# A hybrid decoder step: scan rows kept in SBUF, memory values split from PSUM, earlier scan loads, other PSUM banks

## The chip, the cores and the metric

The kernel runs on one core of a Trainium2 chip. The metric is the device time of one execution in microseconds (us). A median of the runs is compared; the profile is of one further execution.

## The reference, cut to what matters

One layer of a decoder on 1024 prompt tokens and 8 x 4 sample tokens, width 1024, all in float32. A normalized input is projected onto columns for three branches; their outputs are concatenated (3072 wide) and projected back, with a residual and a last norm.

```python
hn = rmsnorm(x, norm_g)
gm_uv, gm_gate, ssm_z, ssm_xbc, ssm_dt, mem_q, mem_gate = split(hn @ w_in)
a_out, v_rows = gmlp_branch(gm_uv, ...)            # gelu, layernorm, 128x128 mixing
a_out = a_out * silu(gm_gate)
b_out, ssm_new, conv_new = mamba2_branch(ssm_z, ssm_xbc, ssm_dt, ...)
c_out = memory_branch(mem_q, mem_gate, mem_k, mem_v)  # 4 heads x 256, 256 memory rows
y = x + concat([a_out, b_out, c_out]) @ w_out
```

`mamba2_branch` is a causal convolution and a scan over chunks of 128 tokens: for each of 16 heads a decay matrix times `C B^T`, times `x dt`, plus the carried state; then a gate with `silu(z)`, a norm over each of two groups of 512 columns, and a gain. For the prompt `mem_k` and `mem_v` are computed from 256 memory rows and are outputs; for the samples they come from a cache, and the scan starts from a given state.

## The kernel before, in words

Every float32 product is made of three products of rounded operands: each operand is split into a high part H (a copy rounded to float32r, mostly on ScalarE) and a low part L (the difference, mostly on VectorE): `split`, lines 121 to 127. TensorE computes HH + HL + LH (`gemm3`, lines 335 to 345).

The order of all instructions is written by hand. The main stream is the large products. Side work is a queue of Python generators (`Side`); after every three products a hook adds a rate (`set_pace`) to a counter, and at each whole number one step of the first generator is written into the program, up to its next `yield`. All engines run their instructions in that order. SP issues nearly all DMAs, GpSimd a few. A DMA that has to wait (for data, or for its buffer) holds what stands behind it on its queue.

The main stream: columns of z, v; then units of 256 columns. A fast unit (`unit`, line 495) is seven products of 512-wide blocks with four k each, 28 hooks; a plain unit (`unit_plain`, line 555) eight, 32 hooks. Six units are convolution columns, then four of q, two of the memory gate (mg), four of the gMLP gate (gg), four of u; then plain units: two of mg and four of the first third of the output projection (written to `y_d`). A weight block is split group by group, three groups ahead (`u_split`, line 441); its low part is left for the next hook (`u_late`, line 452). In each unit the 32 sample columns are products into a bank `U.bank()` (`samp_in`, line 483), copied to `se`, and in the next unit transposed into another bank (`samp_out`, line 470).

PSUM has eight banks of 128x512: three `mm` for the main products, one `acc`, four `sd` for everything beside.

Side chains. `side_chain` (line 1748, begun by `conv_end` in the first q unit): `conv_samples`, `sample_scan` (line 1343; 8 states of 128x1024, each scaled on GpSimd in `s1`, line 1431), a wait for the flag `F_.q` set by `q_there` in the first mg unit, `sample_scores`, `sample_values`, `mem_prep` (line 1649: norm and transposes of the memory rows, H and L stored to `mem_d`), and `gm_prep` (line 1683: spatial weights). `scan_chain` (line 1932) is begun by `scan_open` in the first plain mg unit: `decay_rows` (line 909; rows of `Lraw` through SP, rows of `Rt` through GpSimd), then `scan` (line 1231): 16 chunks (group g, chunk c). For each, `sA` transposes x and B, `sE` makes the decay (a product of Lt and Rt, then ScalarE), `sM` multiplies it by `C B^T`, `sXsplit` splits x times decay (ScalarE, then GpSimd for `xdL`), lines 1201 to 1203 form the state, line 1276 the diagonal part; `gate_norm` gates and norms y; one iteration later `y_T` transposes it into an `sd` bank and `y_T2` scales it (ScalarE, line 1124) and stores it to `yb_d`.

After the plain units: 16 products for keys and values of the memory (blk 0 to 7, two halves each; lines 2070 to 2089). Beside them `loadB` and `splitB` load y from `yb_d`, at most three tiles ahead, and split it into bH and bL; `splitB` is called once per product and twice at every fourth. Values go to `mv_d` and are read back as `vr`, to be split in the attention chain. Then `outproj` (line 1973): 24 products (192 hooks) that add to `y_d`, with `attention` (line 2171) as side chain at pace 0.38, which in the end loads c, x rows, the last gain and y sums for the last stage.

`a_split` (line 1946) splits the gMLP output, four blocks, beside the second plain mg unit: two halves of 128x1024 each, the low parts through `u_late`.

Of the kernel before, what the change touches and what calls it, by code (L numbers as in the profile page):

```python
# [58 lines left out]
def hybrid_step(ctx, tc, x_prompt, x_sample, mem_prompt, state_ssm, state_conv, cache_mem_k,  # L59
# [355 lines left out]
    U.bank = acc_bank  # L415

# [24 lines left out]
    def u_split(u, j):  # L441
# [7 lines left out]
        U.late.append((l, src, h))  # L449
        U.hl[u, j] = (h, l)  # L450

    def u_late():

        while U.late:
            l, src, h = U.late.pop(0)
            DVE.tensor_tensor(out=l, in0=src, in1=rb(h), op=ALU.subtract)  # L456
# [13 lines left out]
    def samp_out():  # L470
# [5 lines left out]
        ps = sd()  # L476
# [78 lines left out]
    def unit_plain(u, X, xs, dst, fin, done, mids=None, func=AF.Copy):  # L555

        nx = u + 1 if u + 1 < len(useq) and useq[u + 1] == useq[u] + 2 else len(useq)
        for j in range(8):
# [12 lines left out]
            if j == 1:  # L571
                samp_out()
# [336 lines left out]
    def decay_rows():  # L909


        bp = b_ctx.enter_context(tc.tile_pool(name="bp", bufs=1, side="right"))
# [184 lines left out]
    SC_ = WS()  # L1097

# [13 lines left out]
    def y_T(y, T, g, t0):  # L1112
        o = VO["ssm_norm_g"] + 4 * g
        ps = sd().rearrange("p (i n) -> p i n", i=4)
        for i in range(4):
            PE.transpose(out=ps[:, i, :T], in_=y[:T, i * 128:(i + 1) * 128], identity=ident[:T, :T])
        return ps, o

    def y_T2(r, T, g, t0, t):

        ps, o = r
        t = t.rearrange("p (i n) -> p i n", i=4)[:, :, :T]
        for i in range(4):
            ACT.activation(out=t[:, i, :], in_=ps[:, i, :T], func=AF.Copy, scale=vecs[:, o + i:o + i + 1])
        return lambda: SP.dma_start(out=yb_d[4 * g:4 * g + 4, :, t0:t0 + T].rearrange("k p t -> p k t"), in_=t)
# [14 lines left out]
    def xk_load(i):  # L1140

        if i < 16:
            g, c = divmod(i, 8)
            tok = slice(c * 128, (c + 1) * 128)
            xk = SC_.p.tile([128, 4, 128], F32, tag="xk", name="xk", bufs=1)
            SP.dma_start(out=xk, in_=xc_d[4 * g:4 * g + 4, :, tok].rearrange("k p t -> p k t"))
            bc = SC_.p.tile([128, 2, 128], F32, tag="bc", name="bc", bufs=2)
# [13 lines left out]
    def sA(i):  # L1161
# [17 lines left out]
        xk_load(i + 1)  # L1179
# [51 lines left out]
    def scan():  # L1231
        sz_load(0)
        xk_load(0)
        lt_make(0)
        lt_make(1)
        for _ in range(4):
            yield
# [8 lines left out]
        for i in range(16):  # L1246
# [46 lines left out]
            if i > 0:  # L1293
                p = S.pop(i - 1)
                gp_, cp_ = divmod(i - 1, 8)
                r = y_T(p.xsD, 128, gp_, cp_ * 128)
# [46 lines left out]
    def sample_scan(sp2):  # L1343
# [87 lines left out]
        def s1(b):  # L1431
# [10 lines left out]
            POOL.tensor_tensor(out=hbt, in0=hbt, in1=decT[:, :, b].unsqueeze(2).to_broadcast([128, 8, 128]), op=ALU.mult)  # L1442
# [305 lines left out]
    def side_chain():  # L1748
# [3 lines left out]
        v_ctx.close()  # L1752
        with tc.tile_pool(name="samp", bufs=1) as p:
# [7 lines left out]
        with tc.tile_pool(name="memp2", bufs=1) as p:  # L1761
            yield from mem_prep(p)
# [19 lines left out]
    U.bank = acc_bank  # L1782

# [134 lines left out]
    def scan_open():  # L1918
# [8 lines left out]
        AB.todo = [(nm, k) for nm in AB.t for k in range(4)]  # L1927
        side.add(scan_chain())
# [3 lines left out]
    def scan_chain():  # L1932
        yield from decay_rows()
        SC_.p = c_ctx.enter_context(tc.tile_pool(name="ssd", bufs=1, side="right"))
        SC_.done = 0
# [10 lines left out]
    def a_split(nm):  # L1946
        def f():
            OA[nm] = operand(*((xT1p, "xT1") if nm == "B12" else (xTp, "x" + nm)))
            for e in range(2):
# [3 lines left out]
                U.late.append((L, src, H))  # L1953
# [47 lines left out]
    def kv_open():  # L2001
# [3 lines left out]
        M.p = m_ctx.enter_context(tc.tile_pool(name="memp", bufs=1))  # L2005
        M.H = M.p.tile([128, KD, 256], F32R, name="memH")
# [26 lines left out]
    mv_d = dpool.tile([2, 128, 1024], F32, name="mv_d")  # L2033
# [36 lines left out]
    for blk in range(8):  # L2070
        wp = w_take(2)
        cs = slice((blk % 4) * 256, (blk % 4) * 256 + 256)
        for i in range(2):
# [8 lines left out]
            else:  # L2082
                SP.dma_start(out=mv_d[i, :, cs], in_=st)
# [12 lines left out]
    opp = opB_ctx.enter_context(tc.tile_pool(name="opp", bufs=1, side="right"))  # L2096
    kv2_ctx = ExitStack()
    kvp2 = kv2_ctx.enter_context(tc.tile_pool(name="kvp2", bufs=1, side="right"))
    vH = kvp2.tile([128, 2, 1024], F32R, name="vH")
    vL = kvp2.tile([128, 2, 1024], F32R, name="vL")  # L2100
# [70 lines left out]
    def attention():  # L2171
# [252 lines left out]
```

## Time and profile before

| | |
|---|---|
| median of 3 runs | 1398.56 us (1397.22 to 1782.47) |
| the profiled execution | 1391.03 us, span 1389.3 us |
| TensorE busy | 1290.4 us (93%), mean granted clock 0.977 |
| VectorE, ScalarE, GpSimd busy | 746.9, 588.2, 361.3 us |
| moved by DMA | 209.15 MB, mean 151 GB/s |

PE is TensorE's products, PEld its weight loads, DVE VectorE, ACT ScalarE, POOL GpSimd, SP the queue that issues DMAs. The granted clock is 1.00 at the upper level. A row's time in square brackets is the idle time of the engine just before the instruction, with what ended it.

### The profile page before, as it was taken

Reading aid. Unit: us, or ns where it says so; the run is one execution under the profiler, and the core shown is the slowest. Engines: PE = TensorE matmul, PEld = TensorE weight load, DVE = VectorE, ACT = ScalarE, POOL = GpSimd, SP = SyncE. Lnnn points to the kernel's source line nnn. Section 1 sums busy time; section 2 is a strip of 40 time slices with the busy share of each in tenths; the row PEclk is TensorE's granted clock in tenths of the full one; section 3 lists DMA queues with packets and bytes.
Section 4 is the critical chain, followed back from the end, with each engine's and each line's share of the span. In section 5 each row is a group of like instructions: output and inputs, shape, how many; then the busy total and the mean of one; then the engine's idle time right before and its main releaser. Section 6 shows DMA issues by size and latency. Waiting matters only on the chain. (4 is left out here: it accounts for less than half of the span.)

```text
span 1389.3 us, 22059 instructions
## 1 busy us (share of the span) xinstructions
PE 1290.4 (93%) x8211; PEld 1084.4 (78%) x8211; DVE 746.9 (54%) x1242; ACT 588.2 (42%) x1172; POOL 361.3 (26%) x387
## 2 busy tenths in 40 slices
PE   8999999999999999997999887888889789998996
PEld 7999998787767676565788665666658789998996
DVE  6112437999745643333676446666564546652543
ACT  6323324554332333212477457645455434331322
POOL 4401623232555310211353422233330000000122
PEclk9999999999999999998999989999999999999999
DMA  7232331323455463745556453334537876657542
GB/s 233 74 96 85 131 94 57 103 93 109 127 167 170 149 206 100 245 133 200 169 172 214 117 181 119 97 109 121 170 97 223 242 215 197 195 157 248 168 141 97
DMA packets 216544, 209.15 MB, mean 151 GB/s; under 512 B 28605, under 2 KB 182289, under 8 KB 215413
## 3 DMA queue, kind: packets, MB, share of 16 engines
q1 hardware_dynamic: 215668, 207.34, 47.9%
q8 instruction: 65, 1.06, 0.3%
q0 software_dynamic: 768, 0.40, 0.2%
q14 instruction: 43, 0.34, 0.1%
HBM read 140.80 MB, written 66.62 MB: 149 GB/s over the span
## 5 line engine op out<-in xcount | busy, mean ns | idle before, releaser
L448 ACT ACTIVATE uh<-wst 128x512 fp32r<-128x512 f32 x80 | 50.2, 627 | 107.9 <-PE ps_mm L340 92.7
L2329 POOL TENSOR_TENSOR xres<-xres,gfin 128x1536 f32<-128x1536 f32 (+3 forms) x6 | 14.4, 2397 | 298.9 <-ACT junk L2323 298.9
L456 DVE TENSOR_TENSOR ul<-wr,uh 128x512 fp32r<-128x512 f32 x84 | 69.8, 831 | 37.0 <-ACT uh L448 36.9
L127 DVE TENSOR_TENSOR wl<-wr,wh 128x512 fp32r<-128x512 f32 (+3 forms) x53 | 50.0, 966 | 63.8 <-ACT wh L124 63.2
L456 DVE TENSOR_TENSOR ul<-wst,uh 128x512 fp32r<-128x512 f32 x80 | 62.6, 783 | 27.3 <-ACT uh L448 27.0
L448 ACT ACTIVATE uh<-wr 128x512 fp32r<-128x512 f32 x84 | 52.4, 624 | 58.5 <-PE ps_mm L340 57.0
L339 PE MATMUL ps_mm<-bH,wh 128*128 128x384 f32 (+1 forms) x192 | 64.0, 333 | 2.7 <-DVE gt L1993 2.7
L341 PE MATMUL ps_mm<-bH,wl 128*128 128x384 f32 (+1 forms) x192 | 62.6, 326 | 0.0
L340 PE MATMUL ps_mm<-bL,wh 128*128 128x384 f32 (+1 forms) x192 | 62.5, 326 | 0.0
L434 POOL TENSOR_TENSOR wst<-wr 128x512 f32<-128x512 f32 x20 | 27.0, 1350 | 114.0 <-DMA wr<-in_w_in_dram 57.8
L339 PE MATMUL ps_mm<-xB22H,uh 128*128 128x512 f32 x128 | 53.3, 416 | 2.1 <-ACT sz_s L1109 2.1
L1012 DVE SCALAR_TENSOR_TENSOR ps_sd<-raw,vecs,ps_sd 128x512 f32<-128x512 f32 x72 | 54.2, 752 | 1.7
L339 PE MATMUL ps_mm<-xT1H,uh 128*128 128x512 f32 x128 | 53.6, 419 | 0.0
L339 PE MATMUL ps_mm<-xB11H,uh 128*128 128x512 f32 x128 | 53.1, 414 | 0.0
L339 PE MATMUL ps_mm<-xB21H,uh 128*128 128x512 f32 x128 | 52.6, 411 | 0.0
L124 ACT ACTIVATE wh<-wr 128x512 fp32r<-128x512 f32 (+3 forms) x60 | 46.6, 810 | 13.6 <-PE ps_mm L341 6.3
L341 PE MATMUL ps_mm<-xT1H,ul 128*128 128x512 f32 x128 | 50.8, 397 | 0.0
L340 PE MATMUL ps_mm<-xT1L,uh 128*128 128x512 f32 x128 | 50.8, 397 | 0.0
L340 PE MATMUL ps_mm<-xB11L,uh 128*128 128x512 f32 x128 | 50.7, 396 | 0.0
L340 PE MATMUL ps_mm<-xB22L,uh 128*128 128x512 f32 x128 | 50.7, 396 | 0.0
L341 PE MATMUL ps_mm<-xB22H,ul 128*128 128x512 f32 x128 | 50.7, 396 | 0.0
L341 PE MATMUL ps_mm<-xB11H,ul 128*128 128x512 f32 x128 | 50.6, 395 | 0.0
(506 smaller groups left out, 4262.0 us busy)
## 6 DMA issues: line engine op xcount, KB each, us to landing
wr<-in_w_in_dram SPq DMA_DIRECT2D x56, 512.0 KB
wr<-in_w_out_dram SPq DMA_DIRECT2D x24, 512.0 KB
kv<-in_cache_mem_k_dram SPq DMA_DIRECT2D x16, 512.0 KB
kv<-in_cache_mem_v_dram SPq DMA_DIRECT2D x16, 512.0 KB
xt<-in_x_prompt_dram SPq DMA_DIRECT2D x8, 512.0 KB
z_d<-gt SPq DMA_DIRECT2D x32, 128.0 KB
v_d<-gt SPq DMA_DIRECT2D x32, 128.0 KB
xc_d<-cd SPq DMA_DIRECT2D x16, 256.0 KB
```

What stands on the lines that cost most here:

```text
L124: ACT.activation(out=H, in_=raw, func=AF.Copy)
L127: leng.tensor_tensor(out=L, in0=raw, in1=rb(H), op=ALU.subtract)
L339: PE.matmul(out=ps, lhsT=lH, rhs=rH, start=(first and k == k0), stop=False)
L340: PE.matmul(out=ps, lhsT=lH, rhs=rL, start=False, stop=False)
L341: PE.matmul(out=ps, lhsT=lL, rhs=rH, start=False, stop=(last and k == k0 + kn - 1))
L434: POOL.tensor_tensor(out=t1, in0=A_(u, 2, 1), in1=A_(u, 2, 2), op=ALU.add)
L448: ACT.activation(out=h, in_=src, func=AF.Copy)
L456: DVE.tensor_tensor(out=l, in0=src, in1=rb(h), op=ALU.subtract)
L1012: DVE.scalar_tensor_tensor(out=ps, in0=raw[:, 512 * h + j:512 * h + j + 512], scalar=cw(ct, j), in1=ps, op0=ALU.mult, op1=ALU.add)
L2329: eng.tensor_tensor(out=t[:, 0:nf, c0:c0 + w], in0=t[:, 0:nf, c0:c0 + w], in1=gc.unsqueeze(1).to_broadcast([128, nf, w]), op=ALU.mult)
```

## The change

1. Memory preparation runs before the sample scan, no longer after the sample values.
2. In `s1` the state is scaled by 64 ScalarE instructions of 128x128 in place of 8 on GpSimd.
3. The pools of the scan are opened in `scan_open`, which also issues the loads of the first two chunks; x rows have two buffers, B and C rows three, each loaded two chunks ahead; two empty steps are gone.
4. `u_late` takes an engine: the low part of the second half of each A block is made on GpSimd.
5. y transposes go to the `acc` bank. In plain units sample products go to a free `mm` bank and their transposes to `acc`.
6. y of group 1, chunks 4 to 7, stays in SBUF (`SC_.y`), is not stored, and is split first. Values of the memory are split from PSUM into vH and vL; `mv_d` is gone.
7. Attention runs at pace 0.43; y sums are loaded before the x rows, one per step.

```diff
     def u_late():
 
         while U.late:
-            l, src, h = U.late.pop(0)
-            DVE.tensor_tensor(out=l, in0=src, in1=rb(h), op=ALU.subtract)
+            l, src, h, eng = U.late.pop(0)
+            eng.tensor_tensor(out=l, in0=src, in1=rb(h), op=ALU.subtract)
...
-        ps = sd()
+        ps = U.bank2()
...
             if j == 1:
+                free = (mmn[0] + 2) % 3
+                U.bank, U.bank2 = lambda: mm_bank(free), acc_bank
                 samp_out()
                 samp_in(u, xs, done)
...
-        bp = b_ctx.enter_context(tc.tile_pool(name="bp", bufs=1, side="right"))
+        bp = SB_.p
...
+        kept = T == 128 and g and t0 >= KEEP * 128
+        if kept:
+            t = SC_.y[t0 // 128] = SC_.yp.tile([128, 512], F32, name=f"y{t0 // 128}")
...
+        if kept:
+            return lambda: None
...
-        xk_load(i + 1)
+        xk_load(i + 2)
...
     def scan():
-        sz_load(0)
-        xk_load(0)
         lt_make(0)
         lt_make(1)
-        for _ in range(4):
-            yield
+        yield
+        yield
         sA(0)
         sE(0, 0)
...
-                r = y_T(p.xsD, 128, gp_, cp_ * 128)
+                r = y_T(p.xsD, 128, gp_, cp_ * 128, acc_bank())
...
-            POOL.tensor_tensor(out=hbt, in0=hbt, in1=decT[:, :, b].unsqueeze(2).to_broadcast([128, 8, 128]), op=ALU.mult)
+            for k in range(8):
+                ACT.activation(out=hbt[:, k, :], in_=hbt[:, k, :], func=AF.Copy, scale=decT[:, k, b:b + 1])
...
         v_ctx.close()
+        with tc.tile_pool(name="memp2", bufs=1) as p:
+            yield from mem_prep(p)
         with tc.tile_pool(name="samp", bufs=1) as p:
             yield from sample_scan(p)
...
-        with tc.tile_pool(name="memp2", bufs=1) as p:
-            yield from mem_prep(p)
         yield from gm_prep()
...
+        SB_.p = b_ctx.enter_context(tc.tile_pool(name="bp", bufs=1, side="right"))
+        SC_.p = c_ctx.enter_context(tc.tile_pool(name="ssd", bufs=1, side="right"))
+        xk_load(0)
+        xk_load(1)
+        sz_load(0)
         side.add(scan_chain())
...
-                U.late.append((L, src, H))
+                U.late.append((L, src, H, POOL if e else DVE))
...
-    ytodo = [(g, c) for c in range(NTILE) for g in range(2)]
+    ytodo = [(1, c) for c in range(KEEP, 8)] + [(0, c) for c in range(NTILE)] + [(1, c) for c in range(KEEP)] + [(1, 8)]
...
+            if g and KEEP <= c < 8:
+                ybs.append((g, c, SC_.y[c].rearrange("p (k t) -> p k t", k=4)))
+                return
...
-                SP.dma_start(out=mv_d[i, :, cs], in_=st)
+                split(ps[:, :256], vH[:, i, cs], vL[:, i, cs], ACT, DVE)
...
-    vr = kvp2.tile([128, 2, 1024], F32, name="vr")
-    for i in range(2):
-        SP.dma_start(out=vr[:, i], in_=mv_d[i])
...
-        for _ in range(3):
-            yield
-        for i in range(2):
-            split(vr[:, i], vH[:, i], vL[:, i], ACT, DVE)
+        for _ in range(5):
             yield
...
-        xres[0] = hp.tile([128, 3, D], F32, name="xres0")
-        x_rows(0)
-        gf.append(hp.tile([128, D], F32, name="gfin"))
-        SP.dma_start(out=gf[0], in_=final_norm_g.unsqueeze(0).to_broadcast([128, D]))
         for i in range(5):
             t = ysum[0, i] = hp.tile([128, 384], F32, tag="ys", name="ys", bufs=5)
             SP.dma_start(out=t, in_=y_d[i, :, 0:384])
+            yield
+        xres[0] = hp.tile([128, 3, D], F32, name="xres0")
+        for j in range(3):
+            SP.dma_start(out=xres[0][:, j], in_=xp_rows[j * 128:(j + 1) * 128, :])
+            yield
...
-    set_pace(0.38)
+    set_pace(0.43)
```

## Rows read from the trace of the kernel before

**Rows 1.** Stretches: busy us and instructions of each engine, clock, DMA share, GB/s.

```profile
392.00:452.00 60.00, 60.00 (x343) 42.92 (x343) 27.05 (x42) 18.34 (x34) 31.39 (x21) 1.00 0.61 179
630.00:660.00 30.00, 20.38 (x103) 15.62 (x102) 12.37 (x17) 9.71 (x18) 5.97 (x10) 0.83 0.53 181
785.00:880.00 95.00, 75.05 (x436) 56.18 (x435) 49.05 (x78) 57.03 (x94) 26.28 (x36) 0.91 0.44 135
880.00:1050.00 170.00, 147.89 (x995) 108.53 (x994) 99.53 (x173) 90.35 (x212) 55.40 (x67) 0.97 0.41 124
1050.00:1145.00 95.00, 79.82 (x549) 77.16 (x547) 44.69 (x68) 43.70 (x83) 0.00 (x0) 0.93 0.81 238
1270.00:1290.00 20.00, 14.72 (x75) 13.85 (x74) 5.71 (x9) 4.13 (x6) 0.00 (x0) 0.83 0.80 267
```

**Rows 2.** TensorE's waits over the span: us in total, times, longest.

```profile
PE ps_sd L1201 <- ACT sz L1124: 11.5, 9, 2.3
PE ps_mm L339 <- ACT wh L124: 9.5, 3, 4.3
PE ps_mm L339 <- DVE gt L1993: 7.4, 2, 4.8
PE ps_sd L1174 <- DMA bc<-bc_d: 7.2, 2, 5.0
```

**Rows 3.** Timeline at the memory preparation: start, us, engine, line; idle before.

```profile
622.77 0.39 PE L339 MATMUL ps_mm<-xB22H,uh 128*128 128x512 f32 x1
...
623.45 0.39 PE L339 MATMUL ps_mm<-xB22H,uh 128*128 128x512 f32 x1
...
631.79 1.06 ACT L303 ACTIVATE xn<-mem 128x1024 f32<-128x1024 f32 x1 [6.33 <-DMA mem<-in_mem_prompt_dram]
...
635.29 1.82 PE L317 MATMUL ps_sd<-ident,xn 128*128 128x128 f32 x8 [2.84 <-issue]
...
651.02 0.59 ACT L1065 ACTIVATE csn<-ps_sd 27x512 f32<-27x512 f32 x1 [7.94 <-DMA mem_d<-memL]
...
655.46 1.08 PE L1713 MATMUL ps_sd<-ident,wsp 128*128 128x128 f32 x4 [6.13 <-DMA wsp<-in_gm_w_spatial_dram]
```

**Rows 4.** Timeline at the opening of the scan.

```profile
786.12 4.42 SPq L943 DMA_DIRECT2D Lraw<-neg_d  x8
...
793.94 0.28 DVE L1156 TENSOR_SCALAR Lt<-Lraw,qmask 128x128 fp32r<-128x128 f32 x1 [5.56 <-DMA Rt<-acc_d]
...
803.16 0.52 POOL L951 DMA_DIRECT2D Rt<-acc_d  x1 [10.57 <-PE ps_sd L1212]
...
807.94 0.47 PE L1212 MATMUL ps_sd<-Rt,Lt 128*128 128x512 f32 x1 [0.48 <-DMA Rt<-acc_d]
```

**Rows 5.** Timeline, one chunk of the scan: y scaled, xdL, state product.

```profile
952.90 1.12 ACT L1124 ACTIVATE sz<-ps_sd,vecs 128x128 f32<-128x128 f32 x4
...
953.38 1.26 POOL L127 TENSOR_TENSOR xdL<-xde,xdH 128x512 fp32r<-128x512 f32 x1
...
954.69 0.50 PE L1202 MATMUL ps_sd<-xdL,BH 128*128 128x512 f32 x1
```

**Rows 6.** Timeline: GpSimd beside VectorE, state scaling, low parts of A.

```profile
441.79 1.91 POOL L1442 TENSOR_TENSOR hb<-hb,decT 128x1024 f32<-128x1024 f32 x1
...
817.44 1.27 POOL L1222 TENSOR_TENSOR MT<-MT,cbm 128x512 f32<-128x512 f32 x1 [2.15 <-ACT MT L1218]
...
817.59 1.27 DVE L127 TENSOR_TENSOR CL<-bc,CH 128x128 fp32r<-128x128 f32 x1 [1.94 <-ACT CH L124]
...
859.74 2.36 DVE L456 TENSOR_TENSOR xB21L<-aB,xB21H 128x1024 fp32r<-128x1024 f32 x2 [4.59 <-ACT xB21H L1952]
...
862.99 0.80 PE L1201 MATMUL ps_sd<-hH,CH 128*128 128x512 f32 x1 [4.72 <-DVE BL L127]
```

**Rows 7.** Timeline beside the key and value products, and behind them.

```profile
1075.81 0.63 ACT L124 ACTIVATE bH<-yb 128x512 fp32r<-128x512 f32 x1 [3.35 <-DMA yb<-yb_d]
...
1123.40 5.64 SPq L2103 DMA_DIRECT2D vr<-mv_d  x2
```

More of the change, by code (lines that the diff above doesn't have):

```diff
@@ L415, in hybrid_step @@
     U.bank = acc_bank
+    U.bank2 = sd
     def u_raw(u):
@@ L448, in u_split @@
         ACT.activation(out=h, in_=src, func=AF.Copy)
-        U.late.append((l, src, h))
+        U.late.append((l, src, h, DVE))
         U.hl[u, j] = (h, l)
@@ L1097, in hybrid_step @@
     SC_ = WS()
+    SC_.y = {}
+    KEEP = 4
     def h3(ap):
@@ L1110, in gate_norm, with y_T @@
         return rstd(pool, ss[:T], T, 512)
-    def y_T(y, T, g, t0):
+    def y_T(y, T, g, t0, ps=None):
         o = VO["ssm_norm_g"] + 4 * g
-        ps = sd().rearrange("p (i n) -> p i n", i=4)
+        ps = (sd() if ps is None else ps).rearrange("p (i n) -> p i n", i=4)
         for i in range(4):
@@ L1144, in xk_load @@
             tok = slice(c * 128, (c + 1) * 128)
-            xk = SC_.p.tile([128, 4, 128], F32, tag="xk", name="xk", bufs=1)
+            xk = SC_.p.tile([128, 4, 128], F32, tag="xk", name="xk", bufs=2)
             SP.dma_start(out=xk, in_=xc_d[4 * g:4 * g + 4, :, tok].rearrange("k p t -> p k t"))
-            bc = SC_.p.tile([128, 2, 128], F32, tag="bc", name="bc", bufs=2)
+            bc = SC_.p.tile([128, 2, 128], F32, tag="bc", name="bc", bufs=3)
             for e in range(2):
@@ L1782, in hybrid_step @@
     U.bank = acc_bank
+    U.bank2 = sd
     g_ctx = ExitStack()
@@ L1933, in scan_chain @@
         yield from decay_rows()
-        SC_.p = c_ctx.enter_context(tc.tile_pool(name="ssd", bufs=1, side="right"))
-        SC_.done = 0
         yield from scan()
@@ L2005, in kv_open @@
         M.p = m_ctx.enter_context(tc.tile_pool(name="memp", bufs=1))
+        SC_.yp = m_ctx.enter_context(tc.tile_pool(name="ykeep", bufs=1))
         M.H = M.p.tile([128, KD, 256], F32R, name="memH")
@@ L2032, in hybrid_step @@
     bL = opB.tile([128, 8, NT], F32R, name="bL")
-    mv_d = dpool.tile([2, 128, 1024], F32, name="mv_d")
+    opp = opB_ctx.enter_context(tc.tile_pool(name="opp", bufs=1, side="right"))
+    kv2_ctx = ExitStack()
+    kvp2 = kv2_ctx.enter_context(tc.tile_pool(name="kvp2", bufs=1, side="right"))
+    vH = kvp2.tile([128, 2, 1024], F32R, name="vH")
+    vL = kvp2.tile([128, 2, 1024], F32R, name="vL")
     mk_o = mem_k_prompt[0, 0].rearrange("m h d -> m (h d)")
@@ L2095, in hybrid_step @@
     yb_ctx.close()
[L2096 to L2100, printed above, removed]
-    vr = kvp2.tile([128, 2, 1024], F32, name="vr")
-    for i in range(2):
-        SP.dma_start(out=vr[:, i], in_=mv_d[i])
     a_ctx = ExitStack()
@@ L2223, in attention @@
             SP.dma_start(out=t, in_=y_d[i, :, 0:384])
+            yield
[3 more added lines that the diff above has]
+            yield
+        gf.append(hp.tile([128, D], F32, name="gfin"))
+        SP.dma_start(out=gf[0], in_=final_norm_g.unsqueeze(0).to_broadcast([128, D]))
         yield
```

## The prediction

> **What bounds the kernel now.** I read the stretches first. TensorE is the bound: between the stretches of [rows 1] it is busy all the time (the first of them, 392 to 452 us, is such a one: 60.00 of 60.00). The other five hold nearly all it loses: idle, 9.6 us in 630:660, 20.0 in 785:880, 22.1 in 880:1050, 15.2 in 1050:1145 and 5.3 in 1270:1290. Second, the granted clock: after most stalls of over two us it falls from the upper level (2.4 GHz) to the lower, and (1 - clock) times the stretch is lost as well: 5.1, 8.6, 5.1, 6.7 and 3.4 us. Idle and clock together are 14.7, 28.5, 27.2, 21.8 and 8.7, some 101 us. The change takes no product off TensorE, so 101 us is a ceiling, and each edit is worth what it takes from the stall of its own stretch. Third, TensorE's waits [rows 2] say what ended the stalls, and the timeline [rows 3 to 7] what is late next. Side work is tied to hooks; a hook is three products, 0.68 us in a fast unit (the first two of [rows 3]), so a step costs 0.68/1.15 = 0.6 us of the main stream at pace 1.15 and 1.2 us at 0.56.
>
> **1. Memory preparation moved from behind the sample values to ahead of the sample scan.** Counted in the code: from `conv_end` to `q_there` there are 8 + 84 + 16 = 108 hooks; the convolution samples and the sample scan use about 90 of them (33 steps at 1.15, 15 at 0.32, 16 at 1.15), and the rest are empty steps that wait for the flag. Memory preparation has 21 steps, 18 hooks: it fits, the scores start where they did, and the last chain ends 18 hooks earlier. In the stretch 630:660 two things go wrong now. ScalarE waits 6.33 us for the memory rows, and TensorE then 2.84 for the transposes of `xn` (with what follows about 4.5 us idle); and the 2 MB store to `mem_d` holds the next pool, so that ScalarE waits 7.94 us for a place for `csn` and TensorE 6.13 us for `wsp` [rows 3]. The second goes: `wsp` is issued when the values' pool is released; it takes 4.4 us to land (the store lets go at 651.0, the use is at 655.46) and the seven steps ahead of its use take about as long, so I leave 1.5 us idle and as much clock. The first only moves: the loads cannot be issued before the convolution pool is left, while TensorE runs on; I expect 5 us idle and 3.4 us clock near 380 us. Gone: 14.7, and about 1 us of a stall on the samples that now has time. Left: 5 + 3.4 + 1.5 + 1.5. **Gain 4 to 5, I take 5** (bounds: 0, all of it moved; 15.7, all hidden). SP: the state loads of the sample scan now stand behind the store of `mem_d`, and the weight loads behind them on the same queue, up to 8 us (the wait of `csn`); the high products are made three groups ahead (12 hooks, 8 us), which just covers it.
>
> **2. State scaling from GpSimd to ScalarE.** Out: 8 operations of 1.91 us [rows 6]. In: 8 x 8 of 128x128, which ScalarE runs at 1.12/4 = 0.28 us each [rows 5], 17.9 us. In 392:452 ScalarE is busy 18.3 of 60 us, so it goes to about 36, in bursts of 2.2 us beside two evictions; TensorE waits for nothing there. **0** (bounds +2 and the rival below).
>
> **3. Scan opened early.** The two stalls for `bc` are 5.0 and 2.2 us [rows 2]; the first load is queued behind eight `Lraw` loads (4.42 us of issue [rows 4]) and a pool release. After the change `bc` and `xk` of two chunks and `sz` are asked for first. But that puts seven issues (about 3.1 us) ahead of the `Lraw` loads, and the first decay product needs all eight of those and the `Rt` rows. By its issue, the first Lt is made some 3 us later than now (793.94 [rows 4]), near 797; TensorE, which gets there 4 hooks (2.7 us) earlier, stalls again, on Lt and Rt instead of bc. The second bc stall falls on the `Rt` load that starts only when the product before it is done (803.16) and lands at 807.94 [rows 4]: late next by nearly as much. **1.5** (bounds -3, the Lraw delay unpaid; +8, both bc stalls and their clock).
>
> **4. Half of the low parts of the A operand on GpSimd.** Now both halves run on VectorE, 2.36 us a block; the small products that the scan needs wait behind them, and TensorE 4.72 us [rows 6]. GpSimd is idle there. One half less is 1.2 us earlier. **1** (bounds -3 and +4.7). By rows, a VectorE subtract of 128x128 took 1.27 us and ended 0.15 us after the GpSimd multiply beside which it started [rows 6]. The Trainium skill, page "SBUF — State Buffer", section "SBUF: two separate sides", says that VectorE operations with two SBUF inputs and GpSimd operations lock one port pair for a whole instruction and exclude each other; the trace agrees. By that rule the four halves would hold VectorE's two-input work about 2.5 us each (twice GpSimd's 1.27 for half the size) where they cost 1.2 before, and the edit would lose up to 5 us; without it, it gains the 1.2.
>
> **5. Other banks for y transposes and sample products.** The largest entry of the waits, 11.5 us in 9, is the state product waiting until ScalarE has scaled the transposed y out of the same bank [rows 2]. It looks like the best part of the change and I give it **0**. In the shown case ScalarE ends at 954.02 (952.90 + 1.12) and the first product can start, but the second needs `xdL`, which GpSimd ends at 954.64, and starts at 954.69 [rows 5]. Six of the nine that I followed look so: the second product starts within 0.1 us of the end of `xdL`. Without the bank the first product starts earlier and the second as now. The sample transposes move to the bank that y now uses and still wait for the same scaling. (Bounds: 0 and 11.5 + 4.)
>
> **6. Four y rows kept in SBUF, memory values split from PSUM.** In 1050:1145 the DMA engines are busy 81% [rows 1]; the yb loads land late, ScalarE stands in front of them (3.35 us in the case shown, three such) and the weight split behind it comes late: 9.5 us of TensorE in 3 stalls [rows 2, 7]. The first four splits now need no load, so the first of the three goes: about 2.4 us, 0.4 behind it and 1.7 of clock, 4.5. The other two keep their pattern (two splits every fourth product, three buffers), but 1 MB of yb loads and 1 MB of `mv_d` stores are gone, about 8 us of traffic at the 238 GB/s of the stretch: I take 4 us more. That is **8.5**. Then SP stands 5.64 us on reading `mv_d` back [rows 7], and the loads for outproj and attention stand behind it: the smaller of the two `gt` waits, 2.6 us [rows 2], a late q split and the clock. All of that goes: **5**. (Bounds of the two: 5, and the stretch's 21.8.) The eight added splits (128x256) replace four of 128x1024 and lie beside products.
>
> **7. Attention pace 0.43, loads of the last stage reordered.** The chain has 73 steps against 65; 73/0.43 = 170 hooks of 192, as 65/0.38 = 171. But its attention part ends at hook 135 instead of 152, so the c and y loads start some 13 us earlier and no longer meet the last `gt` load, for which TensorE waits 4.8 us [rows 2]. Of 8.7 I take **8** (bounds 2 and 8.7): the stall goes, what is late next is the first weight split.
>
> **Sum.** 5 + 0 + 1.5 + 1 + 0 + 8.5 + 5 + 8 = 29. The profiled execution took 1391.03 us (span 1389.3), so 1362 for it. The median of the runs shown, 1398.56, is 7.5 above it; the same 29 off that is about 1369.5 us, which I predict (2.1% less).
>
> **The rivals.**
>
> A. *Only the clean stalls go.* Parts 1, 3, 4 turn into other waits and the yb pattern stays: 4.5 + 5 + 5 of part 7 = 14, so 1384. For it: in parts 1, 3 and 5 a new wait stands ready behind the old one. Against: part 6 takes real traffic away.
>
> B. *The bank does count.* If in most chunks `xdL` comes earlier once the transposes don't hold ScalarE and the samples, parts 3 to 5 give half of their ceilings, 15 us more: 1354. For it: it is the largest wait. Against: the times of [rows 5].
>
> C. *Slower: ScalarE becomes the bound of the sample scan.* Place: the eight states, between evictions and the weight halves on the same in-order queue. Price: if each burst (2.2 us) comes on top of a late split, 8 x (2.2 + 1.7 clock) = 31 us, with two evictions behind it 40: 1369.5 + 31 to 40 = 1401 to 1410. It decides when ScalarE has less than 2.2 us idle within the 12 hooks (8 us) for which the high parts are made ahead. Against: 36 of 60 us busy.
>
> D. *The port rule of part 4*: 5 us lost there instead of 1 gained: 1376.
>
> **How the numbers follow.** Forecast with its neighbours (D lies within) 0.55, own range 1358 to 1380; A 0.22; B 0.16; C 0.07. Two per cent, about what a measurement of this kernel can tell from no change, is 28 us, at 1370.6: the forecast stands on that line. Faster by over 2%: half of the forecast's 0.55 and a little (0.32) and B: 0.48. Slower by over 2% needs more than C's lower price; from C and mishaps 0.05. The rest, 0.47, within. The range for 8 in 10: 1348 to 1391, from beyond B to beyond A.
>
> **What would show it.** Right: no wait of TensorE on `wsp` above 3 us; a stall on `xn` near 380; the state product waiting for `xdL` where it waited for sz, with the scan stretch no shorter than by 5 us; a first scan stall on Rt or Lt; two yb stalls, not three, and a shorter kv stretch; no stall near the change to the last stage. Wrong: TensorE idle between 390 and 470; the scan stretch shorter by 10 or more (B); stalls on uh behind the state scaling (C).

## The result and the profile after

The changed kernel takes 1377.37 us (median of 4 runs, 1375.94 to 1381.83); the kernel before, in the same comparison, 1397.89. One of the four runs behind that median, 1782.47 us, is a slow one and does not count in the ratio, from which the gain is read. The ratio is 0.9874, 95% interval 0.9841 to 0.9907: 1.3% faster, some 17.6 us (13 to 22 by the interval), where 28 were forecast. The profiled execution took 1378.58 us (span 1376.9), 12.4 less than that of before; but before's, at 1391.03, was faster than all its timed runs (1394.0 and up), so 12.4 understates the gain.

The stretches of the changed kernel; columns as in [rows 1].

```profile
372.00:400.00 28.00, 21.74 (x116) 16.76 (x115) 14.70 (x20) 9.60 (x18) 8.58 (x15) 0.88 0.44 163
392.00:452.00 60.00, 59.57 (x332) 42.92 (x331) 32.72 (x51) 30.74 (x74) 22.00 (x24) 1.00 0.65 200
484.00:505.00 21.00, 14.82 (x71) 11.19 (x70) 8.77 (x14) 10.61 (x24) 6.57 (x7) 0.84 0.65 191
630.00:660.00 30.00, 29.20 (x152) 21.90 (x153) 16.05 (x25) 6.09 (x11) 4.87 (x6) 1.00 0.43 125
785.00:880.00 95.00, 68.54 (x415) 50.03 (x414) 53.13 (x79) 59.23 (x100) 38.42 (x41) 0.89 0.46 135
880.00:1050.00 170.00, 149.51 (x1011) 110.84 (x1004) 97.60 (x167) 90.55 (x211) 51.69 (x64) 0.96 0.38 119
1050.00:1145.00 95.00, 85.64 (x618) 82.87 (x617) 53.45 (x90) 47.28 (x98) 0.00 (x0) 0.96 0.74 215
1250.00:1280.00 30.00, 27.21 (x161) 26.25 (x160) 10.49 (x16) 5.30 (x8) 0.00 (x0) 1.00 0.71 225
```

Read it against [rows 1]. 630:660 is healed (9.6 us idle then, 0.8 now). Two stretches near 380 and 490, with 2.2 and 0 us idle and a clock of 1.00 before, lose 6.3 and 6.2 us, and the clock with it. 785:880 is worse: 26.5 us idle against 20.0, clock 0.89 against 0.91. The two late stretches are better (keys and values 9.4 us idle against 15.2; at the last stage 2.8 in 30 us against 5.3 in 20).

TensorE's waits over the whole span, changed kernel (us in total, times, longest):

```profile
PE ps_sd L1212 <- POOL xdL L127: 12.9, 11, 1.4
PE ps_sd L1222 <- DMA Rt<-acc_d: 10.1, 4, 3.2
PE ps_sd L317 <- DVE xn L309: 8.5, 3, 6.3
PE ps_sd L1211 <- ACT xdH L124: 7.3, 9, 1.6
PE ps_acc L479 <- ACT sz L1132: 6.8, 2, 6.5
PE ps_mm L339 <- ACT wh L124: 6.3, 2, 3.3
PE ps_sd L1591 <- POOL wst L436: 5.0, 1, 5.0
PE ps_sd L1222 <- DVE Lt L1166: 3.5, 1, 3.5
PE ps_sd L1184 <- DMA bc<-bc_d: 3.4, 1, 3.4
```

Before, the waits on the same tiles were these:

```profile
PE ps_sd L478 <- ACT sz L1124: 4.1, 2, 2.5
PE ps_sd L1201 <- ACT xdH L124: 3.0, 2, 1.6
PE ps_sd L1202 <- POOL xdL L127: 2.9, 4, 1.1
PE ps_sd L1212 <- DMA Rt<-acc_d: 2.3, 4, 0.8
```

sz on the state product [rows 2] is gone (11.5 before), and xdL and xdH have grown from 5.9 together to 20.2. The weight wait went from three to two. The large gt wait is gone (1.9 in 2 is left). Rt and the samples' transposes (L478, now L479) have grown; the weight sum `wst` and Lt are new.

Single executions differ by several us, so I cut the span at points that every version passes in the same place of its main stream: the sample products (16 in a row) of the first q unit, of the first u unit and of the first plain mg unit, and the first product of the keys, of outproj and of the last stage. Spans between them, in us, worked out from the timelines:

```
                          q to u     u   scan  keys/values outproj  last
before                     324.2 100.1  274.2      66.0     150.6  119.5
after                      323.0 100.1  276.9      59.8     147.1  116.3
mem_back          (1)      324.9 100.1  277.5      59.9     146.8  114.4
states_gpsimd     (2)      325.5 100.1  283.0      60.0     147.3  113.7
scan_late         (3)      324.3 100.0  278.8      61.1     147.0  112.8
a_low_vector      (4)      323.0 100.0  277.3      61.9     146.5  112.3
banks_back        (5)      322.6 100.1  280.1      61.4     146.5  113.0
scan_all_back     (3,4,5)  322.5 100.1  279.5      60.0     146.8  114.7
rows_through_dram (6)      322.2 100.0  276.7      66.1     146.7  114.1
values_through_dram (6)    322.5 100.1  276.8      62.9     151.6  114.2
last_loads_back   (7)      322.0 100.1  279.8      59.5     147.4  119.5
loads_ahead                314.4 100.1  274.0      61.3     146.6  112.2
split_early                322.9 100.1  264.4      60.0     147.2  112.5
loads_and_split            318.8 100.1  259.9      59.2     147.5  111.9
```

The u units, which have no stall, take 100.0 or 100.1 in all fourteen: the products cost the same everywhere, and what differs is stalls and the clock behind them. The scan column shows the scatter: in after and the five versions that leave the scan's code alone (1, 2, both of 6, 7) it is 276.7 to 283.0. Differences of three us there mean nothing. The other spans scatter too, among versions that have the same code in them: q to u 322.0 to 324.3 (after and eight more), keys and values 59.2 to 61.9, outproj 146.5 to 147.5, the last stage 111.9 to 116.3. Only what lies outside these stands out.

### The profile page after: what moved, and what is told of

Same layout as the page of the kernel before. It is cut to its first block, busy times and chain, and to the rows that moved or that the text cites. A ratio compares the mean times of both kernels' runs of the same rounds, so it can differ in the third digit from the quotient of the medians.

```text
span 1376.9 us, 22076 instructions
## 1 busy us (share of the span) xinstructions
PE 1283.8 (93%) x8211; PEld 1078.7 (78%) x8211; DVE 750.8 (55%) x1244; ACT 607.8 (44%) x1244; POOL 353.8 (26%) x383
## 5 line engine op out<-in xcount | busy, mean ns | idle before, releaser
L127 DVE TENSOR_TENSOR wl<-wr,wh 128x512 fp32r<-128x512 f32 (+3 forms) x53 | 51.1, 987 | 63.2 <-ACT wh L124 62.6
L341 PE MATMUL ps_mm<-xB21H,ul 128*128 128x512 f32 x128 | 51.4, 401 | 0.0
L340 PE MATMUL ps_mm<-xB21L,uh 128*128 128x512 f32 x128 | 51.3, 401 | 0.0
L341 PE MATMUL ps_mm<-xT1H,ul 128*128 128x512 f32 x128 | 50.5, 394 | 0.0
```

What stands on the lines that cost most here:

```text
L127: leng.tensor_tensor(out=L, in0=raw, in1=rb(H), op=ALU.subtract)
L340: PE.matmul(out=ps, lhsT=lH, rhs=rL, start=False, stop=False)
L341: PE.matmul(out=ps, lhsT=lL, rhs=rH, start=False, stop=(last and k == k0 + kn - 1))
```

## The experiments

In eight kernels one part of the change is undone; two add something; one undoes three parts, one joins the two additions. A ratio is to the kernel before, to be held against 0.9874. Between one undone kernel and the change the two intervals leave about 0.0045 (6 us), so no single ratio of the eight parts decides; the stalls do, and the spans where they leave their scatter.

**Memory preparation back behind the values.**

```diff
         v_ctx.close()
-        with tc.tile_pool(name="memp2", bufs=1) as p:
-            yield from mem_prep(p)
...
             yield from sample_values(p)
+        with tc.tile_pool(name="memp2", bufs=1) as p:
+            yield from mem_prep(p)
```

> The changed kernel with memory preparation put back behind the sample values (part 1 undone alone). Theory, from the trace of after: the move gained next to nothing, since the 6.26 us on xn at 383.86 and the 4.97 us on the weight sum at 498.94 took the place of the stalls that went; undone, the time stays within 2 us of the change's 1377.4, TensorE's waits for xn and for the weight sum go and a wait of some 6 us on wsp and one of some 3 us on xn near 645 come back. Rival, the prediction: the move was worth 5 us, so 1382.

Measured: 0.9914 (0.9884 to 0.9944). From q to u 324.9 against 323.0. The stalls changed place as both theories had it: wsp 5.99 and xn 2.59 are back, those on xn at 384 and on the weight sum are gone. The spans put the move at 1.9 us, of which 0.6 lies outside the scatter of that span, the ratio at 5.6 with 6 us of uncertainty: small, and not told apart between the two theories. Why small, the changed kernel's timeline shows where the scores begin (GpSimd, SP and TensorE):

```profile
490.48 1.07 SPq L1135 DMA_DIRECT2D yb_d<-yst  x2
...
493.10 0.36 SPq L1560 DMA_DIRECT2D qs<-q_d  x1
...
493.17 2.02 POOL L1563 MEMSET qm<- 128x2304 f32 x1 [7.53 <-PE ps_mm L340]
495.71 0.40 POOL L1564 COPY qm<-qs 128x256 f32<-128x256 f32 x1 [0.51 <-DMA qs<-q_d]
496.06 1.26 POOL L435 TENSOR_TENSOR wst<-wr 128x512 f32<-128x512 f32 x1
497.40 1.27 POOL L436 TENSOR_TENSOR wst<-wst,wr 128x512 f32<-128x512 f32 x1
...
498.94 3.43 PE L1591 MATMUL ps_sd<-ident,kv 128*128 128x128 f32 x15 [4.97 <-POOL wst L436]
```

By the code, the scores' pool takes the sample scan's place, and is free only when the sample y (490.48) is stored. The load of `qs` and GpSimd's memset of `qm` both start 1.6 us after that store was issued; behind the memset and the copy stand the two weight sums that TensorE's main stream needs. One late store so holds SP, GpSimd and, 5 us later, TensorE. (The profile names a product as the memset's releaser; that both waited for the store is read from the code and these times. In `loads_ahead`, below, the memset again starts 1.6 us behind the same store.)

**States scaled on GpSimd again.**

```diff
-            for k in range(8):
-                ACT.activation(out=hbt[:, k, :], in_=hbt[:, k, :], func=AF.Copy, scale=decT[:, k, b:b + 1])
+            POOL.tensor_tensor(out=hbt, in0=hbt, in1=decT[:, :, b].unsqueeze(2).to_broadcast([128, 8, 128]), op=ALU.mult)
```

> The changed kernel with the states scaled by 8 GpSimd multiplies in place of 64 ScalarE instructions (part 2 undone alone). Theory, the prediction: 0, so 1377.4 within 1.5 us, and TensorE without a wait between 410 and 480 either way. Rival: ScalarE's bursts delay a split or the end of the sample scan, and the scores behind it; undone the time falls by 2 us or more.

Measured: 0.9882 (0.9835 to 0.9929); q to u 325.5 against 323.0. No gain by undoing it; in 392:452 of after TensorE is idle 0.4 of 60 us. Nothing that can be told, as forecast. In the profiled execution TensorE was even idle less from q to u than with ScalarE scaling (12.8 us against 15.7 in after), but at a granted clock of 0.96 against 0.98, so a cost of two or three us is not excluded.

**The scan opened late again.** Both pools are opened as before, `xk` has one buffer, `bc` two, the loads run one chunk ahead; there are four empty steps. Of this the cut shows the loads and the steps:

```diff
-        xk_load(0)
-        xk_load(1)
-        sz_load(0)
         side.add(scan_chain())
...
     def scan():
+        sz_load(0)
+        xk_load(0)
         lt_make(0)
         lt_make(1)
-        yield
-        yield
+        for _ in range(4):
+            yield
```

> The changed kernel with the scan's pools and first loads as before (part 3 undone alone). Theory: the early opening turned one stall into three (3.43 on bc, 3.54 on Lt, 2.44 on Rt are 9.4 us, against 5.04 + 2.20 + 0.48 = 7.7 before); undone the time falls by 1 to 3 us, to 1374.4 to 1376.4, with two stalls on bc of about 5 and 2 us. Rival, the prediction: worth 1.5 us, so 1379 when undone. Second rival: the two-chunk lead on x and B, C rows is what counts, and undone each chunk waits for bc: 5 us or more slower.

Measured: 0.9869 (0.9845 to 0.9893). Three stalls became two, 5.00 and 2.48 on bc, as before. The time is the same within what can be told, and no chunk behind the opening waits for bc: the longer lead is not what counts. A shorter span shows more than the whole scan: the first plain mg unit, between its sample products and those of the next, takes 48.8 here and 48.0 in before, but 51.2 in after and 49.3 to 51.1 in the eight other versions that open the scan as after does. There the early opening costs a little, about 2 us.

**Both low halves of A on VectorE.** And, in a kernel of its own, **the banks as before.**

```diff
-                U.late.append((L, src, H, POOL if e else DVE))
+                U.late.append((L, src, H, DVE))
```

> The changed kernel with both low halves of the A blocks on VectorE (part 4 undone alone). Theory: the stall of 6.46 us at 877.91 has its cause here: VectorE's gating multiply took 2.12 us beside GpSimd's half, against a median of 0.69, and its hL subtract 1.75 against 0.69, so ScalarE's scaling of y came late; undone that stall falls below 3 us and the time by 2 to 5 us, to 1372 to 1375. Rival: the stall belongs to the bank that y and the samples now share; it stays near 6 us, VectorE has 4 x 1.2 us more to do, and the time is the same or 1 us more.

```diff
-                free = (mmn[0] + 2) % 3
-                U.bank, U.bank2 = lambda: mm_bank(free), acc_bank
...
-                r = y_T(p.xsD, 128, gp_, cp_ * 128, acc_bank())
+                r = y_T(p.xsD, 128, gp_, cp_ * 128)
```

> The changed kernel with y transposes in an sd bank and the samples' products and transposes in acc and sd as before (part 5 undone alone). Theory: the stall of 6.46 us at 877.91 is a wait for the acc bank that y holds until ScalarE has scaled it; undone it goes or falls below 3 us, while the state product waits on sz again for some 10 us in all where it now waits on xdH and xdL; sum 3 to 6 us faster, 1371.5 to 1374.5. Rival, the prediction: 0, so 1377.4 within 1.5. Second rival: the bank did help the scan; undone it is 4 us or more slower.

Measured: 0.9862 (0.9836 to 0.9888) and 0.9867 (0.984 to 0.9894): neither can be told from the change, and neither theory's cause for the stall of 6.46 us holds alone. TensorE's timeline, low halves on VectorE:

```profile
874.96 0.69 PE L479 MATMUL ps_acc<-ident,se 128*128 128x128 f32 x2 [9.26 <-ACT sz L1132]
```

and with the banks as before:

```profile
874.01 0.76 PE L1220 MATMUL ps_sd<-Rt,Lt 128*128 128x512 f32 x1 [5.71 <-DVE xsD L1305]
...
878.43 0.69 PE L479 MATMUL ps_sd<-ident,se 128*128 128x128 f32 x2 [2.38 <-ACT sz L1130]
```

In the change two stalls stand here, 3.20 on Rt and 6.46: 9.7 us. With one part undone they are one of 9.26, or 5.71 + 2.38. So with the scan opened early the pile-up of the A splits (ScalarE's 2 us of high halves, VectorE's low halves, the gate behind both) costs TensorE 8 to 10 us, whichever instruction stands at the end of it. With the scan opened late the same place costs half of that: one stall of 4.72 in before [rows 6] and in `scan_all_back`, 1.85 + 2.89 in `scan_late`. As far as these runs tell, it matters which chunk the splits meet, and part 3 shifts that. The gain in time is smaller: the second plain mg unit takes 50.5 us in after, 49.6 in `scan_late`, 47.3 in before.

**All three back together.**

> The changed kernel with the scan as before in all three parts (3, 4 and 5 undone together). From the first sample product of the second plain unit to the key and value products the stretch took 274.2 us before and 276.9 after, and 276.7 to 283.0 in the eight kernels with one part undone. Theory: the three parts together are worth nothing or cost up to 3 us; undone together the time is 1374 to 1378, and the stretch within 3 us of 276. Rival, the prediction: together worth 2.5 us, so 1380.

Measured: 0.9881 (0.9847 to 0.9916), 1377.73 us; the scan took 279.5, half a us outside the theory's stretch and inside the scatter. The parts 3 to 5 are together worth nothing that can be told.

**y rows through DRAM, values through DRAM.** All rows stored and loaded back in the old order; and, by itself, the values stored, read back as `vr` and split in the attention chain.

```diff
-    KEEP = 4
+    KEEP = 8
...
-    ytodo = [(1, c) for c in range(KEEP, 8)] + [(0, c) for c in range(NTILE)] + [(1, c) for c in range(KEEP)] + [(1, 8)]
+    ytodo = [(g, c) for c in range(NTILE) for g in range(2)]
```

> The changed kernel with all y rows stored and loaded back, in the old order (the kept rows of part 6 undone alone; the values still split from PSUM). Theory, the prediction: with the kept rows the first of three yb stalls goes, 4.5 us; undone there are three waits behind late yb loads again in the stretch of the key and value products, that stretch is 4 to 6 us longer than the 59.8 us of after, and the time is 1381.4 to 1383.4. Rival: the traffic of the values was the load that mattered; undone the stretch stays within 2 us of 59.8 and the time below 1380.

```diff
-                split(ps[:, :256], vH[:, i, cs], vL[:, i, cs], ACT, DVE)
+                SP.dma_start(out=mv_d[i, :, cs], in_=st)
...
+    for i in range(2):
+        SP.dma_start(out=vr[:, i], in_=mv_d[i])
...
+        for i in range(2):
+            split(vr[:, i], vH[:, i], vL[:, i], ACT, DVE)
```

> The changed kernel with the values stored, read back and split in the attention chain (the value half of part 6 undone alone; the first split of attention is again two steps later in work, not in steps). Theory, the prediction: worth 5 us behind the outproj start (SP's wait, the smaller gt wait, the late q split) and some 4 us through traffic; undone 1382 to 1386. Rival, from the stretches of after: outproj gained 3.5 us in all, and most of that belongs to the order of the last stage's loads; undone the time is within 2 us of 1377.4.

Measured: 0.9896 (0.9855 to 0.9938) and 0.9897 (0.9862 to 0.9932). Here the spans say more than the ratios. Without the kept rows keys and values take 66.1, as before, and all three stalls are back at their old places and sizes (2.42, 2.77 and 4.32 before):

```profile
1077.04 0.38 PE L339 MATMUL ps_mm<-wh,memH 128*128 128x256 f32 x1 [2.51 <-ACT wh L124]
...
1094.25 0.38 PE L339 MATMUL ps_mm<-wh,memH 128*128 128x256 f32 x1 [2.62 <-ACT wh L124]
...
1112.60 0.39 PE L339 MATMUL ps_mm<-wh,memH 128*128 128x256 f32 x1 [4.41 <-ACT wh L124]
```

With the rows kept but the values through DRAM the two stalls that stay are 3.30 and 4.77 (after: 2.94 and 3.32), the stretch 62.9, and behind it the q split is late, for which outproj takes 151.6 in place of 147.1:

```profile
1130.63 0.58 PE L2156 MATMUL ps_sd<-kH,qH 128*128 128x256 f32 x1 [3.71 <-ACT qH L124]
```

So the kept rows (with their order, undone together) are worth 6.3 us in this stretch, 4.2 of them outside its scatter, and the values 4.5 in outproj. The 3.1 that the values seem worth in this stretch is only 1.0 outside its scatter; it is not a sum either, since the stretch gained 6.2 with both. The smaller gt wait of before (2.65 us at 1133.53) comes back in neither kernel, so its cause stays open.

**The last stage's loads and the pace as before.**

```diff
-    set_pace(0.43)
+    set_pace(0.38)
...
+        xres[0] = hp.tile([128, 3, D], F32, name="xres0")
+        x_rows(0)
+        gf.append(hp.tile([128, D], F32, name="gfin"))
+        SP.dma_start(out=gf[0], in_=final_norm_g.unsqueeze(0).to_broadcast([128, D]))
         for i in range(5):
             t = ysum[0, i] = hp.tile([128, 384], F32, tag="ys", name="ys", bufs=5)
             SP.dma_start(out=t, in_=y_d[i, :, 0:384])
...
```

The later loads of the same rows, behind the y sums, are out.

> The changed kernel with attention at pace 0.38 and x rows and the last gain loaded ahead of the y sums (part 7 undone alone). Theory, the prediction: worth 8 us; undone TensorE waits some 5 us for gt near the change to the last stage, its clock falls, and the time is 1385. Rival, from the stretches of after (outproj 3.5 us and the last stage 3.4 us shorter, shared with the values' half of part 6): 3 to 5 us, so 1380.4 to 1382.4.

Measured: 0.9909 (0.9882 to 0.9935), 1385.36 us. The gt stall is back (4.75 before):

```profile
1275.21 0.66 PE L339 MATMUL ps_mm<-cH,wh 128*128 128x384 f32 x1 [4.27 <-DVE gt L2006]
```

The last span is 119.5, that of before; in after it was 116.3, in the other eleven 111.9 to 114.7. The part is worth 3.2 us by the profiled pair and 4.8 to 7.6 against the others, of 8 forecast. Pace and order were undone together; which of them it is was not run.

**Loads and stores given more time.** The memory rows have a pool below the convolution's and are loaded in `conv_end`; eight empty steps stand ahead of the scores; at the opening the order is first chunk, `Lraw`, second chunk, z.

```diff
+    mr_ctx = ExitStack()
+    mrp = mr_ctx.enter_context(tc.tile_pool(name="memrows", bufs=1))
     cvp = v_ctx.enter_context(tc.tile_pool(name="conv", bufs=1))
...
+        mem_rows()
         side.add(side_chain())
...
+        for _ in range(8):
+            yield
         while not F_.q:
...
         xk_load(0)
-        xk_load(1)
-        sz_load(0)
         side.add(scan_chain())
...
     def scan():
+        xk_load(1)
+        sz_load(0)
         lt_make(0)
         lt_make(1)
-        yield
-        yield
+        for _ in range(4):
+            yield
```

> The changed kernel with three loads or waits moved: the memory rows have a pool of their own below the convolution's and are loaded when the convolution samples begin; eight empty steps stand between the sample scan and the scores; at the opening of the scan the first chunk's rows and the Lraw rows go ahead of the second chunk's and of z, and the two empty steps are back. Theory: each of the new stalls is a load or a store that has had too little time (memory rows issued at 373.5 and landed near 379.4; the store of the sample y under the scores' pool; Lraw behind five other loads), so the stalls on xn (6.26), on the weight sum (4.97) and on Lt (3.54) go or fall below 1.5 us, with some 7 us of clock: 10 to 18 us faster, 1360 to 1367. Rival: what is late next stands close behind (rstd and the multiply of xn, the scores' own kv loads, Rt): under 5 us faster, 1372 or more.

Measured: 1372.32 us, 0.9837 (0.9809 to 0.9865), 5 us better by the ratio, with an uncertainty of 6: not clear of noise, and at the rival's bound of 1372. Its profiled execution was its fastest (1363.38), inside the theory's range, so the spans flatter it. They are: q to u 314.4 against 323.0, with 9.9 us idle against 15.7 and the clock at 1.00 against 0.98; and the scan 274.0, below all that left the opening as it is. The first plain mg unit takes 44.1 us, 7 less than in after and 4 less than in before; the units behind it give part of that back. TensorE and GpSimd at the places in question:

```profile
378.35 0.66 PE L317 MATMUL ps_sd<-ident,xn 128*128 128x128 f32 x4 [1.70 <-DVE xn L309]
...
491.51 0.40 POOL L1569 COPY qm<-qs 128x256 f32<-128x256 f32 x1 [3.37 <-DMA qs<-q_d]
...
493.84 0.41 PE L1596 MATMUL ps_sd<-ident,kv 128*128 128x128 f32 x2 [2.21 <-POOL wst L439]
...
784.96 0.50 PE L1225 MATMUL ps_sd<-Rt,Lt 128*128 128x512 f32 x1 [2.58 <-DVE Lt L1169]
```

The stall on xn fell from 6.26 to 1.70, that on the weight sum from 4.97 to 2.21 (what is late next is the load of `qs` itself, in front of which GpSimd stands), that on Lt from 3.54 to 2.58, and bc's 3.43 to 0.45. All three that were named (1.70, 2.21, 2.58) stay above the 1.5 us expected.

**The split of x one step earlier.** This tests the ground on which the banks were valued at nothing.

```diff
             if nx:
+                sXsplit(i + 1)
                 sE(i + 1, 1)
                 sC(i + 1)
             yield
...
-            if nx:
-                sXsplit(i + 1)
             fs = []
```

> The changed kernel with the split of the next chunk's x times decay (xdH on ScalarE, xdL on GpSimd) written one step earlier, ahead of the decay's exponential and of the gate; nothing else moved. It tests the reason given for valuing the banks at nothing: that the state product's second part starts when xdL is done. Theory: TensorE's waits on xdL (12.9 us in 11) and xdH (7.3 in 9) of after go almost wholly, since ScalarE then does not stand before xdH waiting for VectorE's gate product; the scan stretch falls by 10 to 18 us and the time to 1359 to 1367. Rival: the next wait stands right behind (the acc bank, whose y is scaled after the gate, or the decay's exponential on ScalarE): the waits move to sz or MT and the time is within 4 us of 1377.4.

Measured: 1366.36 us, 0.9793 (0.9766 to 0.982), 11 us better than the change, beyond both intervals. The scan took 264.4, 12.5 less. TensorE's waits of this kernel:

```profile
PE ps_sd L1211 <- DVE BL L127: 13.9, 9, 3.1
PE ps_sd L1222 <- DMA Rt<-acc_d: 12.6, 5, 4.2
...
PE ps_sd L1212 <- POOL xdL L127: 0.9, 1, 0.9
```

xdL fell from 12.9 to 0.9 and xdH (7.3) left the list; of these 19.3 us, 12.1 came back as waits on BL (13.9 against 1.8) and 2.5 on Rt. In the scan TensorE was idle 41.2 us against 46.9, and busy 223.2 against 230.0 with the same products at a clock of 0.95 against 0.94: over half of the 12.5 us is not idle time.

**Both additions together.**

> The moved loads and waits and the earlier split together, on the changed kernel. Theory: they take different stalls (352 to 677 and the opening of the scan for the loads, the chunks behind it for the split), so the gains add: by the profiled spans 15.5 and 15.7 us, by the ratios 5 and 11; 16 to 30 us faster than the change's 1377.4, so 1347 to 1361. Rival: at the opening they meet, and behind it the scan is bound by the PSUM banks beside the main products (waits on BL, 13.9 us, and on Rt) whichever way it starts: the split's gain halves, 1362 or more.

Measured: 1359.55 us, 0.9736 (0.9702 to 0.9769), 19 us better than the change, 36.5 better than before, and the fastest kernel of the study. By the ratios the gains add within the noise (5 and 11 alone). By the spans of the profiled executions they do not add in full: q to u is 318.8, 4.2 less than in after where `loads_ahead` had 8.6 with the same code. The idle time there is the same (9.8 and 9.9 us), the clock is not (0.98 and 1.00), so half of those 8.6 was the clock of one execution. The largest wait left is on BL, 19.0 us in 10; whether it is worth anything was not tried.

## Why the prediction came out as it did

The direction was right, the size was not: 28 us forecast, 17.6 measured, inside the range, which was wide (1348 to 1391). The time lies next to rival D's 1376 by chance: with part 4 undone nothing changes that can be told. One reading was wrong at the start: the five stretches hold 72 of the 98.9 us that TensorE is idle in the span, not nearly all (8 lie ahead of 350 us, 11 behind 1290), though no part of the sum hangs on it. By its own steps:

- **Part 1, forecast 5, found about 2 (1.9 by the spans, 5.6 by the ratio, neither clear of noise).** The stall on xn came near 380 as said (6.26 and 3.4 of clock, forecast 5 and 3.4), and wsp fell to 0.8 (forecast 1.5). The step that failed is "it fits, the scores start where they did": 108 hooks less the 90 in use left just the 18 that the preparation takes. The first transposes of the scores came at 498.9 in place of 485.9; the empty steps in which the chain had waited for its flag had also covered, by the times of the two kernels, the store of the sample y and the load of `qs`. Without them GpSimd held the weight sums: 4.97 us and, in 484:505 at clock 0.84, 3.4 of clock. Loads and steps put back took 8.6 and 4.2 us off that span in the two kernels that have them, and 5.8 and 5.9 us off its idle time.
- **Part 2, forecast 0, found 0.** Rival C did not come.
- **Parts 3 to 5, forecast 2.5, found 0 within the scan's scatter.** Part 3: the new stall on Lt came, 3.54 us (at 796.53; forecast near 797), and Rt came next (2.44), but bc stayed late too (3.43), which I had taken to go. Part 4: rival D's mechanism is there (below), but no price of it shows: with both halves on VectorE the stalls at the A splits are 9.26 us against 9.7. Part 5: the reasoning held. Without the bank TensorE waits for xdL, and moving the split took that wait away and 11 us with it. Rival B is out: with the banks back the time is the same within 6 us, where it gave parts 3 to 5 15 more. Whether the banks count once the split is early was not run.
- **Part 6, forecast 8.5 + 5, found 6.2 + 3.5 to 4.5.** Mechanism as said: three yb stalls became two, the late q split and the wait for vr went. The term mis-sized is the "4 us more" from less traffic, half of an estimated 8 with no row for the half: the two stalls left are 2.94 + 3.32 = 6.3 us, where the later two of before had 7.1.
- **Part 7, forecast 8, found 3.2 in the profiled pair, 4.8 to 7.6 against the other versions.** The stall went, as said; 1.69 on gt and 0.93 on a weight split are left in after. The clock of that one execution is part of the rest: the last span scatters by 4 us.

Found in all, by the table: 2 + 0 + 6.2 + 3.5 + 6 = 17.7, with the typical last span and nothing for the scan. That this meets the measured 17.6 is in part luck: the profiled pair alone gives 1.2 - 2.7 + 6.2 + 3.5 + 3.2 = 11.4.

Of the signs listed, these came: wsp under 3, xn near 380, xdL in the place of sz, the scan no shorter, two yb stalls, nothing above 1.7 at the last stage. This one did not: the first scan stall was bc, not Lt.

## What to carry to other kernels

Steps that do nothing can be a cover: before work is moved into them, look up which store, pool release or load lands in that time, and which engine stands in order behind it. When a wait names an instruction, ask what the next instruction needs; here taking away the cause of the largest wait alone was worth nothing, and one line moved ahead of an in-order engine's own wait was worth 11 us. Cut several profiles at the same points of the main stream, and take the scatter of each span from versions that leave it alone: parts of 4 to 6 us show there that whole times can't tell apart, parts of 2 us seldom.

## What the runs showed of the hardware

VectorE with both operands in SBUF and GpSimd did keep each other out, the mechanism of rival D. Timeline of the changed kernel, VectorE and GpSimd:

```profile
872.72 0.68 DVE L1307 TENSOR_TENSOR xsD<-xsD,ps_sd 128x512 f32<-128x512 f32 x1
873.43 2.12 DVE L1112 TENSOR_TENSOR xsD<-xsD,sz 128x512 f32<-128x512 f32 x1
875.47 1.75 DVE L1311 TENSOR_TENSOR hL<-hT,hH 128x512 fp32r<-128x512 f32 x1
...
872.58 2.43 POOL L457 TENSOR_TENSOR xB22L<-aB,xB22H 128x1024 fp32r<-128x1024 f32 x1 [3.92 <-ACT xB22H L1965]
874.97 1.71 POOL L1232 TENSOR_TENSOR MT<-MT,cbm 128x512 f32<-128x512 f32 x1
```

The first, with one operand in PSUM, took its usual 0.68 us inside GpSimd's instruction. The two with both operands in SBUF, 0.69 us in the median, ended 0.54 us after GpSimd's (875.55 against 875.01; 877.22 against 876.68): they ran when it let go, and VectorE lost 2.5 us in this block. GpSimd's second took 1.71 us, for 1.28 in the median. The Trainium skill, page "SBUF — State Buffer", section "SBUF: two separate sides", says that a VectorE operation with two SBUF inputs and a GpSimd operation that reads SBUF take a shared port pair as a lock, each for its whole instruction. The trace agrees.

The same stands in nearly every chunk of the scan, in both kernels. VectorE's subtract for CL (128x128) starts beside GpSimd's multiply and ends 0.14 to 0.16 us after it, for 1.26 to 1.30 us, in 27 of 28 cases of before and after. The one that met no GpSimd operation took 0.29. VectorE and GpSimd in the changed kernel, that one first:

```profile
868.20 0.29 DVE L127 TENSOR_TENSOR CL<-bc,CH 128x128 fp32r<-128x128 f32 x1 [2.35 <-ACT CH L124]
...
892.15 1.27 POOL L1232 TENSOR_TENSOR MT<-MT,cbm 128x512 f32<-128x512 f32 x1 [1.74 <-ACT MT L1228]
892.30 1.28 DVE L127 TENSOR_TENSOR CL<-bc,CH 128x128 fp32r<-128x128 f32 x1 [4.19 <-ACT CH L124]
```

A stall of the same length does not cost the same clock each time. The stretch 975 to 1000 of the changed kernel:

```profile
975.00:1000.00 25.00, 20.77 (x134) 14.37 (x135) 14.50 (x28) 12.78 (x31) 7.25 (x9) 0.93 0.50 148
```

and of the one with the last loads back, whose scan is the same code:

```profile
975.00:1000.00 25.00, 21.92 (x114) 15.36 (x115) 13.12 (x24) 12.18 (x31) 7.24 (x9) 0.80 0.47 135
```

In each a stall on Rt ends near the start (2.39 us at 977.04; 1.99 us at 975.51), and near 995 TensorE waits 1.12 us for xdL. At a granted clock of 0.93 the first loses 1.8 of 25 us to the lower level, the second at 0.80 loses 5.0. In steps of 4 us, the first is below the upper level only behind the stall (0.70 and 0.87 from 976 to 984); the second is lower there (0.52 and 0.63) and falls once more behind the wait for xdL (0.58 from 996 to 1000), where the first stays at 1.00. Over the whole scan, the same code took 276.9 us at 0.94 with 46.9 us idle in after, and 283.0 at 0.92 with 48.0 idle in `states_gpsimd`: most of that difference is clock. So a forecast that gives each stall one price for its clock is good only on the mean.
